# Two-layer hybrid decoder trunk: split weights of the first half kept in device memory, norm shares on another engine, two norms ended earlier

## The chip, the cores and the metric

The kernel runs on one core of one Trainium2 chip. The metric is the device time of one execution in microseconds (us), less is better. The engines named below are TensorE (PE, matmuls, with its weight loads PEld), VectorE (DVE), ScalarE (ACT), GpSimd (POOL) and SyncE (SP, which issues every DMA of this kernel). On-chip memory holds the tiles; device memory holds inputs, outputs and, after the change, some intermediate weights.

## The reference, cut to what matters

One sequence of 1024 tokens, width 1024, two layers. Layer 0 mixes with an S5 state-space block and a stick-breaking attention, layer 1 with a causal pooling; each layer then has a squared-ReLU MLP of width 4096 and a gated per-layer embedding. All in float32.

```python
for i in range(DEPTH):
    if i % 2 == 0:
        h = h + even_mixer(h, ...)     # rms_norm, h @ w_in, S5 and attention, concat @ w_out
    else:
        h = h + pool_mixer(rms_norm(h, ln_mix_odd[j]), pool_w[j], pool_scale[j])
    hn = rms_norm(h, ln_mlp[i])
    h = h + jnp.square(jax.nn.relu(hn @ w_mlp_up[i])) @ w_mlp_down[i]
    gate = jax.nn.sigmoid(rms_norm(h, ln_ple[i]) @ w_ple_gate[i])
    h = h + (p[i] @ w_ple_up[i]) * gate
```

## The kernel before

**Tiles.** Features lie on the 128 partitions, tokens along the free axis, in two halves of 512 tokens (`hf` 0 and 1). An activation is eight tiles of 128x512, a weight a tile of 128x1024 (512 KB).

**Split weights.** A float32 product is made of three matmuls in a reduced format: each operand is a high part and a low part, and `gemm` runs high x high, low x high and high x low, so a weight that serves one half is 24 matmuls of 128x512. The parts are made on the chip by `split`: ACT casts the raw tile to the high part (L448), DVE subtracts it from the raw tile for the low part (L452). `wload` (L464) takes a raw tile (tag "wr", two buffers), loads it by a DMA on SP and splits it into two tiles of another tag, mostly "wh" (eight buffers, so four weights). For a stretch of the S5 work, four of these eight buffers hold its tables. Most weights of the mixers, the first block of each MLP, the gates and the pool are used once for each half, and `wload` runs once for each use: 98 splits of this kind in the profile.

**Stages.** `build` sets the order in which the work is written, by generators that are woven into each other:
- `proj_u`: norm of x and the first four column blocks of the input projection. The norm of half 0 is a sum of squares over eight tiles (`final`, then `norm_add`, L502), whose adds run on POOL ("g"); half 1's run on DVE ("v").
- `kvq(0)`, `kvq(1)`: the other twelve column blocks (`proj`), once per half, two weights ahead, beside the S5 passes (`s5`), which need many small DVE and POOL operations and DMAs of 16 pieces (`M`).
- attention (`att`), the gated S5 output (`glu`) and the output projection (`w_out`, `out_s5`).
- `mlp_all` with `mlp` and `between`: the first block of the MLP by ordinary products, the rest by seven-product (Strassen) blocks, `order7`, whose activations and weights are summed and split separately. `after(p, n)` runs behind product n of a phase; in the last phase of layer 0 it adds the embedding's norm shares of the finished tiles.
- `ple(0, (0,))`, `ple(0, (1,))` (`ple_b`): the embedding of layer 0, half by half, eight gate weights each. Where the norm factor `self.r[hf]` is None, the first step runs `preload` (an activation table) and `norm_end` (PE sum over partitions, `st`, L518, then ACT and DVE) after its gate product.
- `pool(0)`, woven into `ple_b`, then the first MLP step of layer 1 with `pool(1)` woven in, then the MLP and the embedding of layer 1.

**What sets the order.** Every engine works through its own queue in order. The queues are laid out from the written order by a scheduler, with the buffers' reuse as the limit: a load waits until the last reader of the buffer it takes is done. SP's queue is one: a DMA that waits holds up those behind it.

Of the kernel before, what the change touches and what calls it, by code (L numbers as in the profile page):

```python
# [19 lines left out]
P = 128  # L20
# [20 lines left out]
class Kern:  # L41
    def __init__(self, ctx, tc, A):
        self.tc, self.nc, self.A = tc, tc.nc, A

        self.sb = ctx.enter_context(tc.tile_pool(name="sb", bufs=1))
        self.hi = ctx.enter_context(tc.tile_pool(name="hi", bufs=1))
        self.ps = ctx.enter_context(tc.tile_pool(name="ps", bufs=1, space=PSUM))
        self.bufs = dict(t2=3, acc=2, u=26, at=8, wq=4, r0=1, r1=1, wr=2, wh=8, mm=2, z=2, b=2, av=1, st=1)
        self.n = 0
# [414 lines left out]
    def wload(self, src, K, tags=("wr", "wh"), hi_eng="a"):  # L464

        raw = self.t([P, 1024], tags[0], name="wr")
        hi, lo = (self.t([P, 1024], tags[1], F32R, name="w") for _ in range(2))
        self.nc.sync.dma_start(out=raw, in_=src)
        self.split(raw, hi, lo, hi_eng)
        return tuple(t.rearrange("p (k n) -> p k n", k=K) for t in (hi, lo))  # L470
# [90 lines left out]
    def proj_u(self):  # L561
# [14 lines left out]
        for k in range(4):  # L576
            if k == 0:
                for i in range(2):
                    nc.sync.dma_start(out=x[0][0][:, i, :], in_=self.A["x"][0][:, i, :])
                    self.final(0, i, x[0][0][:, i, :], G_EVEN, "g")  # L580
                    for j in range(2):
                        wpart(j, i)
                continue
            load(0, k)
            for i in range(2):
                self.final(0, 2 * k + i, x[0][k][:, i, :], G_EVEN, "g")
# [10 lines left out]
        for k in range(8):  # L597
            self.final(1, k, x[1][k // 2][:, k % 2, :], G_EVEN, "v")
# [224 lines left out]
    def mlp(self, i, f, halves, h, tag="at", up=()):  # L823

        nc, v = self.nc, self.nc.vector
        load = lambda m: self.wload(self.A["w_up"][i, 4 * f + m], 8)
# [21 lines left out]
        for hf in halves:  # L848
            for m in range(8):
                ps = self.p([P, HT], "mm")  # L850
                if m % 2 == 0:
                    dn = self.wload(self.A["w_down"][i, 4 * f + m // 2], 4)
# [294 lines left out]
    def mlp_rest(self, i, h, xq):  # L1147
# [6 lines left out]
        def after(p, n):  # L1154
# [55 lines left out]
    def first_up(self, i):  # L1210
        return [self.wload(self.A["w_up"][i, m], 8) for m in range(2)]
# [49 lines left out]
    def ple(self, i, halves, h):  # L1261
# [8 lines left out]
        def up(at):  # L1270
            if at < len(jobs):
                m, hf = jobs[at]
                if m // 4 not in wu:
                    wu[1] = self.wload(A["w_pu"][i, 1], 2)
# [5 lines left out]
        for at, (m, hf) in enumerate(jobs):  # L1280
            if m + 1 not in w and m < 7:
                w[m + 1] = self.wload(A["w_gate"][i, m + 1], 8)
# [21 lines left out]
    def pool(self, hf, h):  # L1304
# [7 lines left out]
        def start(m):  # L1312
            gi = m // 2
            ps = self.p([P, HT], "av")
            if m % 4 == 0:
                self.pw = self.wload(self.A["pool_w"][m // 4], 4)
# [52 lines left out]
    def build(self):  # L1369
# [9 lines left out]
        ws = self.ahead(2, [lambda c=c: self.wload(self.A["w_in"][c], 8) for _ in range(2)  # L1379
# [43 lines left out]
        ple_b = self.ple(0, (1,), h)  # L1423
        run(steps(ple_b, 1))
# [114 lines left out]
```

## Time and profile before

| | us |
|---|---|
| median of three runs | 2117.95 (2117.68 to 2119.14) |
| the profiled execution | 2119.18 |
| its span in the profile | 2117.4 |
| granted PE clock, mean over the span | 0.981 |
| HBM read / written | 129.28 MB / 4.19 MB |

In a profile row of the chain of waits the numbers are the start and the length in us, then engine, tile and line of the kernel before; a DMA row names what is loaded from where. In a row of operations the numbers after the bar are busy us and the mean of one in ns, then idle time in front of it. In a row of waits they are us in all, times, and the longest. A row of DMAs gives the count, the size and the median us from issue to landing.

### The profile page before, as it was taken

The numbers are of one execution on the slowest core, as the hardware profiler recorded it, in microseconds if no ns is written. First come the engines' busy times: TensorE is split into PE (matmuls) and PEld (weight loads), VectorE is DVE, ScalarE is ACT, GpSimd is POOL, SyncE is SP. The second block draws the span as 40 slices with busy tenths as digits, with TensorE's granted clock in tenths as the row PEclk, the third lists the DMA queues.
The fourth block names the chain that finished last, engine by engine and source line by source line (L and its number), as shares of the span: only waits on it lengthen the run. The fifth ranks groups of instructions, "written<-read, shape, count | busy, mean of one in ns | idle before, by whom it ended". The sixth has DMA issues, their size and how long they took to land.

```text
span 2117.4 us, 24722 instructions
## 1 busy us (share of the span) xinstructions
PE 2030.2 (96%) x9464; PEld 1606.6 (76%) x9464; DVE 1781.6 (84%) x2339; ACT 1176.8 (56%) x1701; POOL 131.3 (6%) x263
## 2 busy tenths in 40 slices
PE   7999899999999999999999999879999999999998
PEld 5777665666677888888888887658888888888886
DVE  8876477888778798989769978988797998879999
ACT  5233478877744645555365655533654656365662
POOL 2678000000000000000000000000000000000000
PEclk9999899999999999999999999989999999999999
DMA  5121111210141210211211131231210211210221
GB/s 174 46 64 49 56 60 50 84 47 31 41 150 50 80 50 30 80 57 36 67 60 40 52 108 60 90 111 59 70 50 30 90 40 40 80 60 31 70 70 60
DMA packets 44741, 136.24 MB, mean 64 GB/s; under 512 B 9552, under 2 KB 10704, under 8 KB 44624
## 3 DMA queue, kind: packets, MB, share of 16 engines
q1 hardware_dynamic: 44624, 134.67, 19.0%
q8 instruction: 74, 1.21, 0.2%
q14 instruction: 43, 0.35, 0.1%
HBM read 129.28 MB, written 4.19 MB: 63 GB/s over the span
## 4 chain that ended last, share of the span: by engine, by line
PE 73%; DVE 18%; ACT 4%; issue 3%; DMA 1%; POOL 0%; SPq 0%; DVEq 0%; ACTq 0%
PE mm L480 26%; PE z L480 15%; PE b L480 13%; PE av L480 7%; PE st L480 7%; DVE rz L720 3%; DVE w L452 2%; DVE zs L724 1%; DVE xgl L532 1%; PE av L750 1%; DVE acc L502 1%; PE z L703 1%; ACT na L716 1%; ACT na L717 1%; DVE win L1335 1%
## 5 line engine op out<-in xcount | busy, mean ns | idle before, releaser
L480 PE MATMUL mm<-xgh,w 128*128 128x512 f32 x880 | 288.9, 405 | 6.9 <-DVE k L642 4.4
L452 DVE TENSOR_TENSOR w<-q,w 128x1024 fp32r<-128x1024 f32 x204 | 247.2, 1219 | 0.2 <-ACT w L448 0.2
L448 ACT CAST w<-q 128x1024 fp32r<-128x1024 f32 x204 | 212.7, 1047 | 35.0 <-PE mm L480 20.4
L448 ACT CAST hsh<-H 128x1024 fp32r<-128x1024 f32 x98 | 102.2, 1046 | 196.7 <-PE st L480 82.5
L480 PEld LDWEIGHTS mm<-xgh,w 128*128 128x128 f32 x880 | 167.9, 194 | 48.4 <-issue 9.7
L480 PE MATMUL z<-xsh,w 128*128 128x512 f32 x576 | 177.7, 390 | 0.0
L480 PE MATMUL mm<-xgl,w 128*128 128x512 f32 x440 | 177.0, 402 | 0.0
L448 ACT CAST w<-wr 128x1024 fp32r<-128x1024 f32 x98 | 102.3, 1047 | 126.8 <-PE mm L480 73.1
L452 DVE TENSOR_TENSOR w<-wr,w 128x1024 fp32r<-128x1024 f32 x98 | 128.9, 1322 | 28.4 <-ACT w L448 12.2
L894 DVE TENSOR_TENSOR q<-q,q 128x1024 f32<-128x1024 f32 x114 | 137.2, 1220 | 17.2 <-DMA q<-in_w_down 11.5
L480 PE MATMUL b<-xsh,w 128*128 128x512 f32 x448 | 137.9, 389 | 0.0
L480 PE MATMUL mm<-hsh,w 128*128 128x512 f32 x448 | 137.9, 389 | 0.0
L448 ACT CAST xsh<-X 128x1024 fp32r<-128x1024 f32 x72 | 75.5, 1051 | 98.2 <-PE st L480 51.2
L452 DVE TENSOR_TENSOR hsl<-H,hsh 128x1024 fp32r<-128x1024 f32 x98 | 119.5, 1220 | 10.7 <-ACT hsh L448 10.7
L480 PEld LDWEIGHTS z<-xsh,w 128*128 128x128 f32 x576 | 108.2, 188 | 22.9 <-issue 0.5
L480 PE MATMUL mm<-xsh,w 128*128 128x512 f32 x400 | 123.6, 389 | 0.0
L452 DVE TENSOR_TENSOR xsl<-X,xsh 128x1024 fp32r<-128x1024 f32 x72 | 87.4, 1222 | 40.9 <-ACT xsh L448 40.5
L480 PE MATMUL z<-xsl,w 128*128 128x512 f32 x288 | 112.1, 389 | 0.0
L720 DVE TENSOR_TENSOR_SCAN rz<-na,rz 128x128 f32<-128x128 f32 (+7 forms) x64 | 84.7, 1347 | 27.0 <-ACT na L717 27.0
L480 PE MATMUL mm<-hidh,w 128*128 128x512 f32 x256 | 89.2, 425 | 18.0 <-DVE w L452 9.4
L452 DVE TENSOR_TENSOR xsl<-xt,xsh 128x512 fp32r<-128x512 f32 x108 | 70.1, 686 | 42.0 <-ACT xsh L448 41.9
L480 PE MATMUL b<-hsh,w 128*128 128x512 f32 x336 | 103.6, 389 | 0.0
(366 smaller groups left out, 4842.9 us busy)
## 6 DMA issues: line engine op xcount, KB each, us to landing
q<-in_w_up SPq DMA_DIRECT2D x56, 512.0 KB, 3.8
q<-in_w_down SPq DMA_DIRECT2D x56, 512.0 KB, 3.6
wr<-in_w_in SPq DMA_DIRECT2D x26, 512.0 KB, 3.6
wr<-in_w_out SPq DMA_DIRECT2D x16, 512.0 KB, 3.5
wr<-in_w_up SPq DMA_DIRECT2D x16, 512.0 KB, 3.5
wr<-in_w_down SPq DMA_DIRECT2D x16, 512.0 KB, 3.5
x<-in_x SPq DMA_DIRECT2D x15, 512.0 KB, 4.8
wr<-in_w_gate SPq DMA_DIRECT2D x15, 512.0 KB, 3.4
```

The costliest lines, as they stand in the source:

```text
L448: nc.scalar.copy(out=hi, in_=src)
L452: e.tensor_tensor(out=lo, in0=src, in1=hi.bitcast(F32), op=ALU.subtract)
L480: self.nc.tensor.matmul(ps, a, b, start=(first and n == 0 and i == 0), stop=(last and n == K - 1 and i == 2), skip_group_check=going)
L502: e.tensor_tensor(out=self.acc[hf], in0=self.acc[hf], in1=sq, op=ALU.add)
L532: self.nc.vector.scalar_tensor_tensor(out=lo, in0=x, scalar=g, in1=hi.bitcast(F32), op0=ALU.mult, op1=ALU.subtract)
L703: nc.tensor.matmul(pz[:, 0:b1 - b0], self.q[hf][pair // 2][rows, pair % 2, i * P:(i + 1) * P], self.k[b0 // HT][pair // 2][rows, pair % 2, ...
L716: nc.scalar.activation(out=na, in_=na, func=AF.Exp)
L717: nc.scalar.activation(out=na, in_=na, func=AF.Ln, bias=1.0)
L720: v.tensor_tensor_scan(out=rz[:, rev], data0=na[:, rev], data1=rz[:, rev], initial=0.0, op0=ALU.add, op1=ALU.add)
L724: v.tensor_tensor(out=zs, in0=zs, in1=rz, op=ALU.subtract)
L750: nc.tensor.matmul(self.avp[64 * o:64 * o + 64, i * P:(i + 1) * P], self.v[kb // 4 * 2 + pair // 2][:, kb % 4, cs], w[:, at * P:(at + 1) * ...
L894: (self.nc.vector if eng == "v" else self.nc.gpsimd).tensor_tensor(out=o, in0=a, in1=b, op=op)
```

## The change

Four things, in the order of the diff:

1. `wload` gets a key. The first load under a key splits as before and then stores the high and the low part to two tiles in device memory (pool `dr`). A later load under the same key fetches both parts straight into the buffers, without a raw tile, a cast or a subtraction. Keys are given to 46 weights that are loaded twice: 12 of `w_in`, 8 of `w_out`, 8 up, 8 down, 7 gates, 1 embedding, 2 pool. That adds 92 stores and turns 46 raw loads into 92 loads of parts, each 512 KB.
2. In `proj_u` the seven adds of half 0's norm go from POOL to DVE, and the raw tiles of column blocks 2 and 3 take buffers of "wq" in place of "wr".
3. The norm of half 0 for the embedding of layer 0 ends behind product 4 of the last MLP phase, with its table load, rather than behind the first gate product.
4. `build` runs one step of `ple_b`, then the table load and the end of the pool's norm for half 0, then the second step; `pool` skips its own.

```diff
+        self.dr = ctx.enter_context(tc.tile_pool(name="dr", bufs=1, space=bass.MemoryType.DRAM))
+        self.kept = {}
...
+    def wload(self, src, K, tags=("wr", "wh"), keep=None):
+
+        if keep in self.kept:
+            parts = [self.t([P, 1024], tags[1], F32R, name="w") for _ in range(2)]
+            for t, d in zip(parts, self.kept[keep]):
+                self.nc.sync.dma_start(out=t.bitcast(F32), in_=d)
+        else:
+            raw = self.t([P, 1024], tags[0], name="wr")
+            parts = [self.t([P, 1024], tags[1], F32R, name="w") for _ in range(2)]
+            self.nc.sync.dma_start(out=raw, in_=src)
+            self.split(raw, *parts)
+            if keep is not None:
+                self.kept[keep] = []
+                for t, e in zip(parts, "hl"):
+                    name = "_".join(str(x) for x in keep) + e
+                    d = self.dr.tile([P, 1024], F32, tag=name, name=name, bufs=1)
+                    self.nc.sync.dma_start(out=d, in_=t.bitcast(F32))
+                    self.kept[keep].append(d)
+        return tuple(t.rearrange("p (k n) -> p k n", k=K) for t in parts)
...
-                    self.final(0, i, x[0][0][:, i, :], G_EVEN, "g")
+                    self.final(0, i, x[0][0][:, i, :], G_EVEN)
...
-            w.append(self.wload(self.A["w_in"][j], 8, ("wr", ("at", "wq")[j - 2])))
+            w.append(self.wload(self.A["w_in"][j], 8, ("wq", ("at", "wq")[j - 2])))
...
-                w = self.wload(self.A["w_out"][4 * part + n // 2], 4, ("wr", tag))
+                w = self.wload(self.A["w_out"][4 * part + n // 2], 4, ("wr", tag), ("out", part, n // 2))
...
+            if n == 4:
+                self.preload()
+                self.norm_end(0)
             if n == 2:
-                self.r = [None, None]
+                self.r[1] = None
...
-            if m == 0:
+            if m == 0 and self.r[hf] is None:
                 self.norm_end(hf)
...
         ple_b = self.ple(0, (1,), h)
+        run(steps(ple_b, 1))
+        self.preload()
+        self.norm_end(0)
         run(steps(ple_b, 1))
         pool = self.pool(0, h[0])
```

The other keys (`w_in` in `build`, up, down, `first_up`, `w_pu`, gate, pool) are given in the same way as that of `w_out`.

**DVE at the start.** The rows are DVE's instructions in order, with the line, the operation and out<-in; `s5blk` are the small S5 tables, `xgl` the low part of the normed x, `at` and `w` low parts of weights, `acc` and `sq` the norm's sum and a tile of squares. Line numbers after the change are 15 to 20 higher. Before:

```order
L452 TENSOR_TENSOR at_84<-wr_82,at_83 128x512
L532 SCALAR_TENSOR_TENSOR xgl_87<-x_71,gain,xgh_86 128x512
L452 TENSOR_TENSOR at_81<-wr_79,at_80 128x512
L452 TENSOR_TENSOR at_84<-wr_82,at_83 128x512
L209 MEMSET s5blk_379 128x16
L210 MEMSET s5blk_379 128x16
L83 CAST identb<-ident 128x128
L532 SCALAR_TENSOR_TENSOR xgl_89<-x_72,gain,xgh_88 128x512
```

After the change, from the same subtraction on:

```order
L455 TENSOR_TENSOR at_86<-wr_84,at_85 128x512
L547 SCALAR_TENSOR_TENSOR xgl_89<-x_73,gain,xgh_88 128x512
L517 TENSOR_TENSOR acc_98<-acc_98,sq_109 128x512
L455 TENSOR_TENSOR at_83<-wr_81,at_82 128x512
L455 TENSOR_TENSOR at_86<-wr_84,at_85 128x512
L547 SCALAR_TENSOR_TENSOR xgl_91<-x_74,gain,xgh_90 128x512
L517 TENSOR_TENSOR acc_98<-acc_98,sq_121 128x512
L547 SCALAR_TENSOR_TENSOR xgl_91<-x_74,gain,xgh_90 128x512
L517 TENSOR_TENSOR acc_98<-acc_98,sq_126 128x512
L455 TENSOR_TENSOR w_153<-wr_151,w_152 128x1024
L455 TENSOR_TENSOR w_159<-wr_157,w_158 128x1024
```

The adds into `acc` stand between the weights and the normed tiles, the two whole-weight subtractions of blocks 2 and 3 have moved up, and the S5 tables begin behind them.

**SP in the input projection.** Before, the second half's loads are raw (`wr`), behind the sixteen pieces of an S5 block:

```order
L364 DMA M_1262<-kt_1247 16x4x32 x2
L364 DMA M_1262<-kt_1247 16x4x16 x2
L468 DMA wr_1534<-in_w_in 128x1024
L468 DMA wr_1660<-in_w_in 128x1024
L468 DMA wr_1740<-in_w_in 128x1024
L468 DMA wr_1812<-in_w_in 128x1024
```

After the change, first the place where half 0's last parts are stored between raw loads (`in_4h` is the stored high part of column block 4), then that of the second half's loads:

```order
L483 DMA in_15h<-w_1194 128x1024
L476 DMA wr_1341<-in_w_in 128x1024
L483 DMA in_15l<-w_1195 128x1024
L476 DMA wr_1426<-in_w_in 128x1024
L483 DMA in_4h<-w_1342 128x1024
L483 DMA in_4l<-w_1343 128x1024
```

```order
L367 DMA M_1678<-kt_1663 16x4x32 x2
L367 DMA M_1678<-kt_1663 16x4x16 x2
L472 DMA w_1788<-in_9h 128x1024
L472 DMA w_1789<-in_9l 128x1024
L472 DMA w_1858<-in_10h 128x1024
L472 DMA w_1859<-in_10l 128x1024
L472 DMA w_1946<-in_11h 128x1024
L472 DMA w_1947<-in_11l 128x1024
```

A store stands behind the split of its weight, and raw loads written later stand behind the store; in the second half each weight is two loads.

**PE at the embedding of half 1 and the first pooled half.** `st` is the sum over partitions that ends a norm, `av` the pool's product, `mm` a gate product. Before, the norm's row comes behind the second gate weight and the pool's first six products:

```order
L480 MATMUL mm_10204<-xgl_9583,w_10127 128x512
L480 MATMUL av_10247<-xgh_9772,w_10249 128x512
L480 MATMUL av_10247<-xgh_9772,w_10250 128x512
L480 MATMUL av_10247<-xgl_9773,w_10249 128x512
L480 MATMUL av_10247<-xgh_9772,w_10249 128x512
L480 MATMUL av_10247<-xgh_9772,w_10250 128x512
L480 MATMUL av_10247<-xgl_9773,w_10249 128x512
L518 MATMUL st_10260<-acc_9782,one 128x512
L480 MATMUL mm_10311<-xgh_9584,w_10199 128x512
```

After the change it stands between the first and the second gate weight, without a product of the pool ahead:

```order
L495 MATMUL mm_10220<-xgh_9640,w_10183 128x512
L495 MATMUL mm_10220<-xgh_9640,w_10184 128x512
L495 MATMUL mm_10220<-xgl_9641,w_10183 128x512
L533 MATMUL st_10285<-acc_9848,one 128x512
L495 MATMUL mm_10299<-xgh_9642,w_10216 128x512
L495 MATMUL mm_10299<-xgh_9642,w_10217 128x512
L495 MATMUL mm_10299<-xgl_9643,w_10216 128x512
```

Then pool(1), beside the first up weights of the MLP of layer 1. Before, one up weight lies between the MLP's norm and the pool's first product (the row of the norm is 25 rows earlier):

```order
L480 MATMUL mm_10772<-xgh_10299,w_10712 128x512
L480 MATMUL mm_10772<-xgl_10300,w_10711 128x512
L480 MATMUL av_10803<-xgh_10186,w_10805 128x512
L480 MATMUL av_10803<-xgh_10186,w_10806 128x512
L480 MATMUL av_10803<-xgl_10187,w_10805 128x512
L480 MATMUL av_10803<-xgh_10186,w_10805 128x512
L480 MATMUL av_10803<-xgh_10186,w_10806 128x512
L480 MATMUL av_10803<-xgl_10187,w_10805 128x512
L518 MATMUL st_10816<-acc_10196,one 128x512
L480 MATMUL mm_10858<-xgh_10293,w_10717 128x512
```

After the change the pool's first product follows that norm's row directly:

```order
L495 MATMUL mm_10871<-xgh_10434,w_10799 128x512
L495 MATMUL mm_10871<-xgl_10435,w_10798 128x512
L533 MATMUL st_10856<-acc_10438,one 128x512
L495 MATMUL av_10902<-xgh_10272,w_10903 128x512
L495 MATMUL av_10902<-xgh_10272,w_10904 128x512
L495 MATMUL av_10902<-xgl_10273,w_10903 128x512
L495 MATMUL av_10902<-xgh_10272,w_10903 128x512
L495 MATMUL av_10902<-xgh_10272,w_10904 128x512
L495 MATMUL av_10902<-xgl_10273,w_10903 128x512
L533 MATMUL st_10913<-acc_10282,one 128x512
L495 MATMUL mm_10955<-xgh_10428,w_10808 128x512
```

The 24 matmuls of the second up weight moved from in front of the pool's first product to behind it.

More of the change, by code (lines that the diff above doesn't have):

```diff
@@ L462, in act @@
         return out
[L464 to L470, printed above, removed]
+    def wload(self, src, K, tags=("wr", "wh"), keep=None):
[16 more added lines that the diff above has]
+        return tuple(t.rearrange("p (k n) -> p k n", k=K) for t in parts)
     def gemm(self, ps, w, m, x, first=True, last=True, turn=0, going=False):
@@ L585, in proj_u @@
             for i in range(2):
-                self.final(0, 2 * k + i, x[0][k][:, i, :], G_EVEN, "g")
+                self.final(0, 2 * k + i, x[0][k][:, i, :], G_EVEN)
         w = [tuple(t.rearrange("p (k n) -> p k n", k=8) for t in hl[1:]) for hl in w]
         for j in (2, 3):
-            w.append(self.wload(self.A["w_in"][j], 8, ("wr", ("at", "wq")[j - 2])))
+            w.append(self.wload(self.A["w_in"][j], 8, ("wq", ("at", "wq")[j - 2])))
         self.consts()
@@ L597, in proj_u @@
         for k in range(8):
-            self.final(1, k, x[1][k // 2][:, k % 2, :], G_EVEN, "v")
+            self.final(1, k, x[1][k // 2][:, k % 2, :], G_EVEN)
         for j in range(4):
@@ L825, in mlp @@
         nc, v = self.nc, self.nc.vector
-        load = lambda m: self.wload(self.A["w_up"][i, 4 * f + m], 8)
+        load = lambda m: self.wload(self.A["w_up"][i, 4 * f + m], 8, keep=("up", i, m))
         n_up = 2 if tag == "wh" else 4
@@ L851, in mlp @@
                 if m % 2 == 0:
-                    dn = self.wload(self.A["w_down"][i, 4 * f + m // 2], 4)
+                    dn = self.wload(self.A["w_down"][i, 4 * f + m // 2], 4, keep=("down", i, m // 2))
                 self.gemm(ps, dn, m % 2, hid[hf])
@@ L1210, in first_up @@
     def first_up(self, i):
-        return [self.wload(self.A["w_up"][i, m], 8) for m in range(2)]
+        return [self.wload(self.A["w_up"][i, m], 8, keep=("up", i, m)) for m in range(2)]
     def between(self, i, solo):
@@ L1273, in up @@
                 if m // 4 not in wu:
-                    wu[1] = self.wload(A["w_pu"][i, 1], 2)
+                    wu[1] = self.wload(A["w_pu"][i, 1], 2, keep=("pu", 1))
                 ups.append(self.p([P, HT], "zb"[at // 2 % 2]))
@@ L1281, in ple @@
             if m + 1 not in w and m < 7:
-                w[m + 1] = self.wload(A["w_gate"][i, m + 1], 8)
+                w[m + 1] = self.wload(A["w_gate"][i, m + 1], 8, keep=("gate", m + 1))
             hk = h[hf][m]
@@ L1315, in start @@
             if m % 4 == 0:
-                self.pw = self.wload(self.A["pool_w"][m // 4], 4)
+                self.pw = self.wload(self.A["pool_w"][m // 4], 4, keep=("pool", m // 4))
             wt = [t[:, 2 * (gi % 2):2 * (gi % 2) + 2] for t in self.pw]
             self.gemm(ps, wt, m % 2, xg[2 * gi:2 * gi + 2])
-            if m == 0:
+            if m == 0 and self.r[hf] is None:
                 self.norm_end(hf)
@@ L1377, in build @@
         self.k, self.q, self.v = [[], []], [[], []], []
-        ws = self.ahead(2, [lambda c=c: self.wload(self.A["w_in"][c], 8) for _ in range(2)
+        ws = self.ahead(2, [lambda c=c: self.wload(self.A["w_in"][c], 8, keep=("in", c)) for _ in range(2)
                             for c in (8, 9, 10, 11, 12, 13, 14, 15, 4, 5, 6, 7)])
```

## Prediction

> **What bounds the kernel now.** I read three views in this order: the page with the busy shares and the chain that ended last, then the busy time by stage, then the chain and the waits inside the stages that are not saturated.
>
> ```profile
> span 2117.4 us, 24722 instructions
> PE 2030.2 (96%) x9464; PEld 1606.6 (76%) x9464; DVE 1781.6 (84%) x2339; ACT 1176.8 (56%) x1701; POOL 131.3 (6%) x263
> PE 73%; DVE 18%; ACT 4%; issue 3%; DMA 1%; POOL 0%; SPq 0%; DVEq 0%; ACTq 0%
> ```
>
> TensorE (PE) is busy for 96% of the span, but only 73% of the chain is PE; VectorE (DVE) holds 18% and ScalarE (ACT) 4%. So there are stretches in which the PE goes at the pace of the others. The view by stage says where (columns: start and end, length, then busy us and instructions of PE, weight load, DVE, ACT, POOL, then granted clock, DMA share, GB/s):
>
> ```profile
> 0.00:80.00 80.00, 62.97 (x248) 48.53 (x249) 72.31 (x254) 32.53 (x50) 29.68 (x53) 0.97 0.35 120
> 80.00:250.00 170.00, 159.31 (x929) 121.80 (x927) 112.64 (x158) 55.58 (x84) 100.74 (x203) 0.93 0.20 62
> ...
> 420.00:590.00 170.00, 157.36 (x912) 110.53 (x911) 139.00 (x156) 130.91 (x205) 0.00 (x0) 0.98 0.15 51
> 590.00:660.00 70.00, 65.79 (x277) 52.97 (x276) 62.09 (x78) 31.09 (x42) 0.00 (x0) 0.95 0.36 126
> 660.00:1270.00 610.00, 610.00 (x2687) 503.68 (x2686) 519.80 (x602) 339.67 (x457) 0.23 (x2) 1.00 0.18 58
> 1270.00:1350.00 80.00, 72.36 (x297) 56.14 (x296) 72.91 (x109) 44.71 (x74) 0.67 (x6) 0.96 0.20 67
> 1350.00:1410.00 60.00, 48.59 (x172) 34.89 (x171) 54.05 (x77) 26.14 (x46) 0.00 (x0) 0.88 0.28 92
> 1410.00:1460.00 50.00, 45.19 (x176) 35.11 (x175) 43.45 (x52) 17.83 (x22) 0.00 (x0) 0.90 0.35 121
> 1460.00:2100.00 640.00, 637.87 (x2808) 526.48 (x2807) 560.21 (x656) 354.04 (x479) 0.00 (x0) 1.00 0.16 55
> ```
>
> From 660 to 1270 the PE is never idle: 610.00 us over 2687 matmuls is 0.227 us each at a clock of 1.00. From 1460 on it is the same. Nothing in these 1250 us can be won by freeing DVE or ACT. Measured by 0.227 us a matmul, the others lose: 590 to 660, 277 matmuls are worth 63 us, so 7 are lost; 1270 to 1350, 297 are worth 67, 13 lost; 1350 to 1410, 172 are worth 39, 21 lost; 1410 to 1460, 176 are worth 40, 10 lost. DVE is at 72.91 of 80 and 54.05 of 60 in the two stages that lose most: there it is the bound. Before 590 the shapes are mixed, and I go by the chain.
>
> **The change, price of one reload.** A first use is loaded raw, cast on ACT and subtracted on DVE. 46 second uses lose both operations and get two 512 KB loads instead of one: 12 of the input projection, 8 each of the output projection, up and down, 7 gates, 1 of the embedding, 2 of the pool.
>
> ```profile
> L448 ACT CAST w<-wr 128x1024 fp32r<-128x1024 f32 x98 | 102.3, 1047 | 126.8 <-PE mm L480 73.1
> L452 DVE TENSOR_TENSOR w<-wr,w 128x1024 fp32r<-128x1024 f32 x98 | 128.9, 1322 | 28.4 <-ACT w L448 12.2
> wr<-in_w_in SPq DMA_DIRECT2D x26, 512.0 KB, 3.6
> out_h<-x SPq DMA_DIRECT2D x15, 256.0 KB, 2.0
> 36.00:38.00 2.00, 2.00 (x11) 1.65 (x10) 2.00 (x5) 2.00 (x5) 0.00 (x0) 1.00 1.02 418
> ```
>
> Of these 98 splits, 46 go: 46 x 1.05 = 48 us of ACT and 46 x 1.32 = 61 us of DVE. What it costs: today a split waits for a free pair of buffers with its raw tile already landed, so a weight is ready 1.05 + 1.32 = 2.4 us after its buffers come free; afterwards the whole transfer comes behind that moment. If the two halves follow each other strictly it is 2 x 3.6 = 7.2 us; if the second only adds its bytes, 3.6 + 0.52 MB at the 418 GB/s of the last row, 1.25, gives 4.9. A weight is 24 matmuls, 24 x 0.227 = 5.44 us of PE. So where one other weight covers the reload, the price lies between 0 and 7.2 - 5.44 = 1.8 us for each, 83 us for 46. By the nearest row, the single load's 3.6, I take the lower end for most, and four reloads at 1.8, **+7 us**: those for which the order leaves no other weight ahead (the pool's first weight, which now follows one norm row after the gemm whose buffers it takes over, and those of the input projection while four of the eight buffers hold S5 tables).
>
> The Trainium skill, page "DMA: Bandwidth & Descriptors", section "Anatomy of one DMA — SWDGE (gpsimd) path", fits a transfer by 2.0 us + bytes / 436 GB/s. As an estimate, that page gives 4.4 us for both halves together and no stall, and a total 7 us lower than mine; its 3.2 us for one half is below the 3.6 us of the row, so the measurement decides and the term stays.
>
> **The start, 0 to 80.**
>
> ```profile
> L502 POOL TENSOR_TENSOR acc<-acc,sq x7: 1266/1327/1938, 8.3 to 21.8; 128x512 f32<-128x512 f32 x7
> L502 DVE TENSOR_TENSOR acc<-acc,sq x77: 673/685/693, 34.5 to 2013.9; 128x512 f32<-128x512 f32 x77
> 12.37 1.21 DVE s5blk L122
> ...
> 22.43 1.18 DVE s5blk L131
> 24.96 0.17 DVE L124 TENSOR_SCALAR s5blk<-s5blk 128x16 f32<-128x16 f32 x1
> PE mm L480 <- DVE k L642: 4.4, 1, 4.4
> ```
>
> Between 12.37 and 22.43 the chain holds six small S5 operations of about 1.2 us, while POOL runs its seven adds; after the adds the same form takes 0.17. Moving the adds removes 6 x 1.03 = 6 us of stretching and adds 7 x 0.685 = 4.8 us to DVE. In the new order 25 fewer of the small operations stand ahead of the first key result, for which the PE waits 4.4 us: 25 x 0.17 = 4.2. Two raw tiles of this projection that now come from another tag lose a wait for an earlier split; where DVE is the bound that brings nothing. Net 4.8 - 6 - 4.2, about **-5 us**. Bounds: -10 (the adds fall in gaps) and +5 (DVE waited for x under the stretched operations anyway).
>
> **Second half of the input projection and attention, 80 to 590.**
>
> ```profile
> 185.03 1.14 DVE w L452
> 206.32 0.94 ACT w L448
> 208.03 1.27 DVE w L452
> 265.12 1.12 DVE w L452
> 283.94 1.22 DVE w L452
> ...
> 581.38 1.14 DVE w L452
> 582.54 3.50 DMA wr<-in_w_out
> ```
>
> The first five pieces of the chain are splits of second uses, 5.7 us; I take **-4**, since behind each stands another DVE operation. At the end of the attention a split and the raw load behind it are 4.6 us of the chain, and splits also stand in front of attention copies in ACT's queue: **-5**. Bounds together: -14, and +29 if all 16 reloads there cost 1.8.
>
> **Output projection and first MLP blocks, 590 to 660.** 12 second uses leave DVE, 12 x 1.32 = 16 us of 62.09, but only the 7 lost PE microseconds can come back: **-5**, bounds -7 and +22 (12 x 1.8). The embedding of half 0 lies in the saturated stretch; its earlier norm, which issues no DMA, is worth 0 there, because PE has other matmuls to run.
>
> **Embedding of half 1 with the pool, 1270 to 1460.**
>
> ```profile
> 1282.39 1.23 DVE w L452
> 1307.54 3.38 DMA wr<-in_w_gate
> 1350.04 4.71 DMA wr<-in_w_down
> 1448.06 4.50 DMA wr<-in_w_down
> PE av L480 <- DVE pz L1326: 4.9, 3, 4.5
> L1291 ACT ACT_TABLE_LOAD x3 | 3.8, 1283 | 0.1
> 1410.00:1460.00 50.00, 13.26 (x11) 0.90 0.35 121
> ```
>
> In the first stage DVE sheds six splits that fall inside it, 6 x 1.22 = 7.3 us; the norm, now taken before the second step, removes the 4.5 us wait for pz from the front but only hands the PE on to a full DVE. With two more table loads of 1.28 us on an ACT that idles 35 of 80 us (cost nothing; 2.6 if in the norm's own path), **-7**, bounds -13 and +14 (8 reloads). In the second the chain waited 4.71 us for a raw down load, held back by splits that had not freed its buffer; two pool and two up splits go and free it earlier: **-4**, bounds -12 and +7. In the third, of the 13.26 us of splits in 11 operations (last row, DVE busy in this stage at line 452) most are second uses, yet the load of 4.50 us comes with them: **-5**, bounds -10 and +11.
>
> **The sum.** -5 - 4 - 5 - 5 - 7 - 4 - 5 = -35, +7 for reloads = -28. The profiled execution took 2119.2 us for its span of 2117.4, so 2091; the median of the runs is 2118.0, 1.2 below it, and gives **2090 us**.
>
> **The rivals.**
>
> *The reloads come late (slower).* The buffer pair comes free when its last matmul ends, and two transfers then stand before the next weight. For it: 7.2 us exceed the 5.44 of one weight. Against it: eight buffers hold four weights, so outside the S5 stretch two or three weights lie between. It eats the gain of 35 from 35 / 1.8 = 19 of 46 reloads on; with 30 of them, 54 us, it is 2118 - 35 + 54 = 2137.
>
> *The stores hold things up (slower).* Each first use is now followed by two 512 KB stores on the same queue, which wait for the split, and later raw loads stand behind them; the pair of buffers is also not free before both have landed. A 256 KB store took 2.0 us, so two of 512 KB last at least 4.0 and, at the load's 3.6, 7.2: the same 1.8 over the PE's 5.44. With 30 of 46: again 54 us, less the net 28, so 2144; it decides from 28 / 1.8 = 16. Against it: with PE saturated the DMA share is 0.16 to 0.18, so the room is there, and a first use is gone through in no less than 5.44 us anyway. The 2.0 us of the 256 KB store, below the 3.6 of a 512 KB load, shows no long tail at a store's end. The Trainium skill, in the same page and section ("DMA: Bandwidth & Descriptors", "Anatomy of one DMA — SWDGE (gpsimd) path"), says that a transfer's completion is slowest where the target is device memory, which speaks for this rival; that row bears it out so little that its chance is small.
>
> *Only the DVE-bound stages gain.* The splits before 660 had slack that the chain doesn't show, their reloads cost what they save; 1270 to 1350 and 1410 to 1460 remain, -7 - 5 = -12: 2106.
>
> *The PE takes it up.* The splits on the chain are replaced by the next DVE operation, and reload stalls offset the rest: within 4 us of 2118.
>
> *More than the sum.* In 1270 to 1460 the PE was busy for 166 us with matmuls worth 146 at full clock, at granted clocks of 0.96, 0.88 and 0.90. If fewer gaps raise the clock, up to 20 us more: 2070.
>
> **How the numbers follow.** Forecast 0.44 (2078 to 2100), only the DVE-bound stages 0.19, more than the sum 0.14, the PE takes it up 0.10, reloads late 0.08, stores 0.05. The range runs from 2066 to 2120: it takes in the DVE-bound case and the unchanged one, and leaves out the two slow cases and the far end of the gain, under 0.2. The bounds of the single terms all added reach further on both sides, but no one mechanism puts all of them at one end. About 0.2%, 4.2 us, is what a measurement of this kernel can tell from no change: faster 0.77, same 0.10, slower 0.13.
>
> **What would show it.** Right: splits at 52 for 98; from 1270 on, the stages that sum to 190 us take about 174; no DMA wait of 4.7 at the first down block; the small S5 operations near 12 us at 0.17; first keys some 5 us sooner. Wrong: PE or DVE waits ended by a reload in many places, a row of PE waits of 1 to 2 us in the second projection, or raw loads that are issued late behind stores. If the stretch before 590 ends no sooner and only the later one does, the DVE-bound rival holds.

## The result and the profile after

| kernel | median us | lowest to highest | runs | ratio to before, 95% interval |
|---|---|---|---|---|
| before, beside these runs | 2118.14 | 2115.79 to 2119.14 | 6 | |
| changed | 2099.77 | 2092.86 to 2100.92 | 6 | 0.9904 [0.989, 0.9919] |

The change saves 18.4 us, 28 were forecast. The profiled execution is the fastest of the six, 2092.86 us for a span of 2090.8, and so 7 us away from the median; the others are within 1.2 us of each other. Where those 7 us lie is part of what follows.

The page of the changed kernel (the lines that answer to those of before):

```profile
span 2090.8 us, 24861 instructions
PE 2018.7 (97%) x9464; PEld 1602.4 (77%) x9464; DVE 1740.8 (83%) x2300; ACT 1134.4 (54%) x1658; POOL 116.2 (6%) x256
HBM read 153.40 MB, written 52.43 MB: 98 GB/s over the span
PE 79%; DVE 14%; ACT 4%; issue 2%; SPq 1%; DMA 0%; POOL 0%; DVEq 0%; ACTq 0%
wr<-in_w_in SPq DMA_DIRECT2D x14, 512.0 KB, 5.7
```

PE's share of the chain went from 73% to 79%, DVE's from 18% to 14%: as meant, splits left the path. The price is in the other rows: 48 MB more are written (52.43 against 4.19) and 24 MB more read, and a raw load of the input projection, now sharing the queue with stores, takes 5.7 us to land where it took 3.6 (3.7 in `no_keep_in` below, which neither stores nor reloads the input projection's weights).

The splits that are left, from the groups of line 455 (count, then shortest, median and longest in ns, first and last start):

```profile
L455 DVE TENSOR_TENSOR w<-wr,w x52: 1198/1221/6278, 14.1 to 1394.4; 128x1024 fp32r<-128x1024 f32 x52
```

98 became 52. The median is 1.22 us, before as after; the 1.32 that the forecast used is a mean, raised by a few long ones. Then the waits of PE that the reloads end (us in all, times, longest), whole span:

```profile
PE mm L495 <- DVE s5blk L214: 6.5, 1, 6.5
...
PE mm L495 <- DMA w<-in_9h: 1.9, 1, 1.9
...
PE av L495 <- DMA w<-pool_0h: 1.7, 1, 1.7
...
PE av L495 <- DMA w<-pool_0l: 0.8, 1, 0.8
...
PE mm L495 <- DMA w<-in_9l: 0.5, 1, 0.5
```

PE waits for only two of 46 reloads, 1.9 + 0.5 and 1.7 + 0.8, 4.9 us in all. Both are where the forecast put them: the pool's first weight and one of the input projection.

For the stages I take marks that both kernels have. Before, the first key result, the first operation of the Strassen blocks, the first and last pooled output, the last add of the first MLP block (first and last start in each row):

```profile
L642 DVE TENSOR_TENSOR k<-mm,r x8: 677/682/691, 77.7 to 223.8; 128x512 f32<-128x512 f32 x8
L925 DVE SCALAR_TENSOR_TENSOR xt<-X,X x96: 681/684/692, 653.6 to 1908.7; 128x512 f32<-128x512 f32 x96
L1326 DVE SCALAR_TENSOR_TENSOR pz<-av,gain,r x16: 740/745/753, 1290.2 to 1400.3; 128x512 f32<-128x512 f32 x16
L854 DVE TENSOR_TENSOR x<-x,mm x32: 661/685/690, 572.4 to 1474.2; 128x512 f32<-128x512 f32 x32
```

and after:

```profile
L657 DVE TENSOR_TENSOR k<-mm,r x8: 676/684/692, 72.9 to 223.0; 128x512 f32<-128x512 f32 x8
L940 DVE SCALAR_TENSOR_TENSOR xt<-X,X x96: 680/684/693, 637.6 to 1881.5; 128x512 f32<-128x512 f32 x96
L1344 DVE SCALAR_TENSOR_TENSOR pz<-av,gain,r x16: 737/746/752, 1273.8 to 1378.7; 128x512 f32<-128x512 f32 x16
L869 DVE TENSOR_TENSOR x<-x,mm x32: 660/682/690, 563.3 to 1447.0; 128x512 f32<-128x512 f32 x32
```

Lead of the changed kernel at these marks: 4.8 us at the first key, 16.0 at the Strassen blocks, 16.4 at the first pooled output, 21.6 at the last, 27.2 at the last add, and from there on it stays within 1 us of that. The same marks and a few more, read in each profile, give the stages (us):

| stage | before | changed | changed, again | stored parts only | no stored parts | norms undone |
|---|---|---|---|---|---|---|
| to the first key | 77.7 | 72.9 | 73.1 | 77.7 | 72.0 | 71.8 |
| to the last query | 235.5 | 234.7 | 234.5 | 239.6 | 234.7 | 234.8 |
| to the end of attention | 276.1 | 271.8 | 276.2 | 274.6 | 285.8 | 271.9 |
| to the last output projection | 25.9 | 24.9 | 24.9 | 25.0 | 25.8 | 24.9 |
| to the first Strassen operation | 38.4 | 33.3 | 33.3 | 33.3 | 38.5 | 33.3 |
| to the first Strassen result | 102.6 | 101.2 | 101.4 | 101.2 | 101.6 | 101.4 |
| to the last embedding output, half 1 | 594.4 | 588.8 | 588.4 | 589.9 | 594.2 | 589.8 |
| to the last pooled output | 49.7 | 51.1 | 53.1 | 46.8 | 51.4 | 46.8 |
| to the last add of the first MLP block | 73.9 | 68.3 | 69.5 | 68.6 | 73.2 | 68.7 |

The rows from 25.9 down repeat from kernel to kernel; the two above them do not: the attention of one and the same program took 271.8 and 276.2.

### The profile page after: what moved, and what is told of

Read it like the earlier page. It is cut to its first block, busy times and chain, and to the rows that moved or that the text cites. A ratio compares the mean times of both kernels' runs of the same rounds, so it can differ in the third digit from the quotient of the medians.

```text
span 2090.8 us, 24861 instructions
## 1 busy us (share of the span) xinstructions
PE 2018.7 (97%) x9464; PEld 1602.4 (77%) x9464; DVE 1740.8 (83%) x2300; ACT 1134.4 (54%) x1658; POOL 116.2 (6%) x256
## 3 DMA queue, kind: packets, MB, share of 16 engines
HBM read 153.40 MB, written 52.43 MB: 98 GB/s over the span
## 4 chain that ended last, share of the span: by engine, by line
PE 79%; DVE 14%; ACT 4%; issue 2%; SPq 1%; DMA 0%; POOL 0%; DVEq 0%; ACTq 0%
PE mm L495 29%; PE z L495 15%; PE b L495 13%; PE av L495 7%; PE st L495 7%; DVE rz L735 3%; DVE zs L739 1%; PE av L765 1%; PE z L718 1%; DVE w L455 1%; ACT na L731 1%; PE z L432 1%; PE z L505 1%; DVE win L1353 1%; ACT na L732 1%
## 5 line engine op out<-in xcount | busy, mean ns | idle before, releaser
L495 PE MATMUL mm<-xgh,w 128*128 128x512 f32 x880 | 283.9, 401 | 13.5 <-DVE s5blk L214 6.5
L495 PE MATMUL z<-hsh,w 128*128 128x512 f32 x336 | 104.0, 390 | 0.0
L495 PEld LDWEIGHTS mm<-xgl,w 128*128 128x128 f32 x440 | 84.2, 191 | 19.3 <-DVE xgl L547 1.4
L495 PEld LDWEIGHTS mm<-hsh,w 128*128 128x128 f32 x448 | 84.1, 188 | 17.5
```

The source lines that it names most:

```text
L495: self.nc.tensor.matmul(ps, a, b, start=(first and n == 0 and i == 0), stop=(last and n == K - 1 and i == 2), skip_group_check=going)
```

## The experiments

Two theories stood against each other. Mine: the stored parts carry the gain, the start some 5 us, the norms next to nothing. The rival: start and norms carry it, and the reloads cost what the splits did. The runs stand in one table; all but the first six of the changed kernel were made in three groups, each with its own runs of before (44 together).

| kernel | median us | runs | ratio to before, 95% interval | mean clock | mean us at clock 0.983 |
|---|---|---|---|---|---|
| before, in the three groups | 2119.9 | 44 | | 0.9809 | 2116.7 |
| changed | 2099.8 | 6 | 0.9904 [0.989, 0.9919] | 0.9830 | 2098.9 |
| after_again | 2100.3 | 5 | 0.9904 [0.9888, 0.9921] | 0.9820 | 2098.2 |
| no_keep | 2119.9 | 12 | 1.0 [0.9987, 1.0013] | 0.9798 | 2115.3 |
| keep_only | 2101.9 | 5 | 0.9911 [0.9894, 0.9928] | 0.9824 | 2100.3 |
| no_keep_in | 2094.1 | 4 | 0.9875 [0.9856, 0.9894] | 0.9852 | 2096.6 |
| keep_in_only | 2121.5 | 12 | 1.0008 [0.9993, 1.0023] | 0.9792 | 2115.0 |
| in_store_only | 2101.5 | 6 | 0.9928 [0.9909, 0.9946] | 0.9817 | 2101.6 |
| norms_undone | 2088.2 | 5 | 0.9865 [0.9844, 0.9885] | 0.9856 | 2093.8 |
| norms_undone_2 | 2092.5 | 6 | 0.986 [0.9833, 0.9887] | 0.9852 | 2095.2 |
| no_in_no_pool | 2100.5 | 6 | 0.9913 [0.9893, 0.9932] | 0.9825 | 2099.7 |
| norms_undone_no_in | 2092.5 | 4 | 0.9862 [0.9834, 0.9889] | 0.9855 | 2096.0 |
| late_norm_undone | 2094.5 | 4 | 0.9874 [0.9851, 0.9898] | 0.9840 | 2095.8 |
| pool_adds | 2105.2 | 6 | 0.9922 [0.9901, 0.9943] | 0.9825 | 2103.8 |

The last column: every run states the mean clock granted to the PE. Within the kernels' own runs the time falls by 1.41 us for each 0.001 of clock (correlation -0.93 over all runs, each kernel's mean taken off). Each kernel's mean is moved along that line to 0.983. This takes out the scatter, but also whatever of the clock belongs to a kernel; the medians hold both. The clock is stated to 0.001, so differences of 1 to 2 us in this column are not to be relied on.

### The changed kernel again: where the 7 us lie

No edit.

> The changed kernel, unaltered. The first six times were 2092.86 for the profiled execution and 2099.73 to 2100.92 for the other five. If the profiled one had a higher granted clock by chance (0.987 against 0.981 to 0.983), this run's times scatter between 2092 and 2101 and follow the clock; if it was another placement or chip, they stay near one value, and the profile shows in which stage the 7 us lie.

It came to 2100.3, profile included (2098.2 us of span, clock 0.981). Up to the last query the two profiles are equal (307.6 us); then the attention takes 271.8 in one and 276.2 in the other. One stretch of it in the first profile (PE, PEld, DVE, ACT, POOL busy, then granted clock, DMA share, GB/s):

```profile
500.00:520.00 20.00, 18.17 (x105) 13.67 (x105) 17.11 (x21) 16.05 (x25) 0.00 (x0) 1.00 0.00 1
```

and in the second:

```profile
500.00:520.00 20.00, 19.81 (x102) 14.56 (x101) 15.91 (x21) 15.74 (x25) 0.00 (x0) 0.85 0.00 1
```

The same program, the same DMA silence, a clock of 1.00 or 0.85. The stage table has the 7 us in three stages in which the PE has gaps, 4.4 in the attention, 2.0 in the pool and 1.2 behind it, and in each the second profile has the lower clock (0.97 for 0.99, 0.87 for 0.93, 0.93 for 0.95). What sets the clock was not tried. The first profile was a lucky one; a sum made from it alone would have said that 28 was hit to within 2.

### Stored parts alone, and all but the stored parts

`no_keep` takes the keys away, `keep_only` takes all else away:

```diff
+        keep = None
         if keep in self.kept:
```

```diff
-                    self.final(0, i, x[0][0][:, i, :], G_EVEN)
+                    self.final(0, i, x[0][0][:, i, :], G_EVEN, "g")
...
-            w.append(self.wload(self.A["w_in"][j], 8, ("wq", ("at", "wq")[j - 2])))
+            w.append(self.wload(self.A["w_in"][j], 8, ("wr", ("at", "wq")[j - 2])))
...
-            if n == 4:
-                self.preload()
-                self.norm_end(0)
             if n == 2:
-                self.r[1] = None
+                self.r = [None, None]
...
-        run(steps(ple_b, 1))
-        self.preload()
-        self.norm_end(0)
         run(steps(ple_b, 1))
```

> Keeps the start and the two norm moves, but every use is loaded raw and split again. My theory, that the stored parts carry most of the gain: slower than the changed kernel by 13 to 25 us, so 2110 to 2118, or 0 to 8 faster than before. The rival, that start and norms carry it and the reloads only cost what they save: within 4 us of 2100.

> The kernel before with the stored parts alone: adds on POOL, raw tiles of blocks 2 and 3 in their old tag, norms where they were. My theory: 10 to 20 us faster than before, 2098 to 2108, since the start's 5 us and what the norms bring are missing. The rival: within 4 us of before, 2118.

2119.9 and 2101.9: without the stored parts the change gives nothing measurable, with them alone all but 2 us of it. At equal clock the stored parts are worth 16.8 us with the rest (2115.3 against the 2098.5 between the two sets of the changed kernel) and 16.4 without it (2116.7 against 2100.3). The stage table says where: with stored parts 33.3 for 38.4 up to the Strassen blocks, 588.4 to 589.9 for 594.4 up to the end of the embedding, 46.8 for 49.7 in the pool, 68.6 for 73.9 behind it. The rival is out. But if start and norms were worth 5 us or more, `no_keep` should have shown it, and the start alone is ahead by 5.7 at the first key there. Something gives it back.

### The norms

`norms_undone` is the changed kernel with the third and the fourth part of the diff above taken back; `late_norm_undone` takes back only the fourth (that in `build`):

```diff
         run(steps(ple_b, 1))
-        self.preload()
-        self.norm_end(0)
-        run(steps(ple_b, 1))
         pool = self.pool(0, h[0])
```

> The changed kernel with both norms ended where they were before. The forecast gave them nothing in the saturated stretch and the removal of one wait of 4.5 us in front of a full VectorE. My theory: 0 to 4 us slower than the changed kernel, 2100 to 2104. The rival, that they are what makes room for the reloads in the later stages: 8 us slower or more.

> The kernel with both norms where they were, a second time, on another chip. The first gave 2088.2 in the median, 12 us under the changed kernel, of which its profile shows 3 to 5 us between the first saturated block and the end of the pool; the rest went with a higher granted clock (0.986 against 0.982). If the clock is chance: 2091 to 2097. If it belongs to the kernel: 2086 to 2091.

> The changed kernel with only the later norm, the one between the first two steps of the embedding of half 1, back where it was; the earlier one stays behind product 4. If the later one costs the 3 to 5 us, by what it does to the order behind it: 2088 to 2096, and the profile has about 636 us from the first saturated block to the end of the pool. If the earlier one does: 2098 to 2101 and about 640 us.

2088.2 and 2092.5 against 2100: I had expected the opposite sign. The norm moves cost the kernel 7 to 12 us in the medians and 4 at equal clock. With only the later one undone it is 2094.5. From the first Strassen result to the last pooled output the profiles have 639.9 and 641.5 us with both moves, 636.6 and 636.9 without, 637.0 with only the later undone: 3 to 5 us, and the later move has nearly all of them.

The loss shows in the second pooled half. The view of the last stage but one, changed kernel:

```profile
1327.60:1378.70 51.10, 42.34 (x162) 30.78 (x162) 43.23 (x63) 23.99 (x42) 0.00 (x0) 0.93 0.46 164
```

changed kernel, again:

```profile
1331.80:1384.90 53.10, 45.38 (x161) 32.91 (x161) 43.22 (x62) 24.05 (x42) 0.00 (x0) 0.87 0.44 159
```

norms undone, and the later norm undone:

```profile
1327.90:1374.70 46.80, 40.76 (x168) 30.39 (x166) 42.49 (x61) 22.43 (x40) 0.00 (x0) 1.00 0.45 164
```

```profile
1337.20:1384.10 46.90, 40.86 (x168) 30.45 (x166) 42.59 (x63) 22.47 (x40) 0.00 (x0) 1.00 0.47 166
```

The busy time of DVE is the same to 1 us (42.5 to 43.2), so DVE was not relieved of work; the clock is 1.00 without the move and 0.93 or 0.87 with it. The order in time at that place, changed kernel, PE and then DVE (start, length):

```profile
1332.96 1.02 PE L533 MATMUL st<-acc,one 128*128 128x512 f32 x2
1335.70 0.49 PE L495 MATMUL av<-xgh,w 128*128 128x512 f32 x1 [1.72 <-DMA w<-pool_0h]
1336.97 0.50 PE L495 MATMUL av<-xgh,w 128*128 128x512 f32 x1 [0.78 <-DMA w<-pool_0l]
...
1338.23 1.10 PE L533 MATMUL st<-acc,one 128*128 128x512 f32 x2
1340.12 0.73 PE L495 MATMUL mm<-xgh,w 128*128 128x512 f32 x2 [0.79 <-DVE relu L855]
```

```profile
1321.85 1.29 DVE L1367 SCALAR_TENSOR_TENSOR x<-win,x 128x512 f32<-128x512 f32 x2
...
1338.65 0.69 DVE L528 TENSOR_TENSOR r<-r,ra 128x512 f32<-128x512 f32 x1
...
1346.51 0.74 DVE L1344 SCALAR_TENSOR_TENSOR pz<-av,gain,r 128x512 f32<-128x512 f32 x1
```

and norms undone:

```profile
1325.92 1.12 PE L533 MATMUL st<-acc,one 128*128 128x512 f32 x2 [0.95 <-DVE acc L517]
1333.49 1.12 PE L533 MATMUL st<-acc,one 128*128 128x512 f32 x2 [0.96 <-DVE ra L526]
1335.57 0.70 PE L495 MATMUL mm<-xgh,w 128*128 128x512 f32 x2 [0.96 <-DVE relu L855]
```

```profile
1315.11 0.69 DVE L1364 SCALAR_TENSOR_TENSOR x<-win,x 128x512 f32<-128x512 f32 x1
...
1333.93 0.69 DVE L528 TENSOR_TENSOR r<-r,ra 128x512 f32<-128x512 f32 x1
...
1343.38 0.74 DVE L1341 SCALAR_TENSOR_TENSOR pz<-av,gain,r 128x512 f32<-128x512 f32 x1
```

With the move, PE's order there is: the products of the first two up weights (48 matmuls from 1315.33 on), the sum for the MLP's norm (the first `st`), the pool's first six products, the sum for the pool's norm, and then the product of the third up weight. Without the later move, in both kernels that lack it, the MLP's sum stands between the first and the second up weight, and the pool's first products stand behind both sums. So the reading of pool(1) in the section on the change was wrong: the `mm` rows behind the pool's sum wait for a `relu`, which reads an earlier product, and so are those of the third up weight. The second did not move behind the pool's product, it moved in front of the MLP's sum.

What is late is the norm factor `r` of the MLP. The first row of DVE in each view is the last pooled `x` of half 0: it ends at 1323.14 with the move and at 1315.80 without. The sum needs it and stands 7 us later, at 1332.96 for 1325.92, and the factor comes at 1338.65 for 1333.93. In both kernels the third up product waits for a `relu` that needs this factor, and starts at 1340.12 for 1335.57. Counted from the last embedding output, it starts 12.3 to 13.9 us on in all six profiles with the later move and the later weights stored, and 7.6 to 7.7 us on in all five that have these weights stored without the later move. The 5 us between them are about the loss of the stage (51.1 to 54.3 for 46.8 to 47.0). That the first pooled half ends later because its pool begins one gate step later is likely and was not tried, nor was why the scheduler lays it out so. The lower clock comes with it; its share was not separated. What the move saves at its own place, 1.1 us up to the embedding's end (588.8 for 589.9 with the stored parts alone), is less than this.

### The pool's reload

The rival for the last point was the reload itself. `no_in_no_pool` loads the pool's weights raw again, and has no keys for the input projection either:

```diff
+        keep = None if keep and keep[0] in ("in", "pool") else keep
         if keep in self.kept:
```

> The changed kernel without the keys of the input projection and of the pool, whose first reload the PE waited for, 1.7 and 0.8 us. If that stall is on the path and two splits more are not: 1 to 3 us faster than without the input keys alone, 2091 to 2093. If VectorE's full stage is the bound there, the two splits put back cost 2 us and it is the same or slower, 2094 to 2097.

2100.5, no better than the changed kernel. The stage of the pool, 54.3 us here, is longer still:

```profile
1332.90:1387.20 54.30, 44.40 (x161) 32.67 (x161) 45.33 (x65) 26.25 (x44) 0.00 (x0) 0.87 0.37 134
```

DVE has 2 us more to do and the clock is at 0.87. The wait for the reload is gone, and the third up product starts as late as before, 12.3 us into the stage, with a longer wait for `relu` in its place:

```profile
1345.23 1.22 PE L496 MATMUL mm<-xgh,w 128*128 128x512 f32 x2 [1.80 <-DVE relu L856]
```

`late_norm_undone` keeps the reload, does not wait for it, and has 46.9 us. So what costs is the late norm factor, not the reload.

### The keys of the input projection

`no_keep_in` leaves out those twelve keys, `keep_in_only` has only them, `in_store_only` stores the parts but loads raw in the second half, `norms_undone_no_in` has neither those keys nor the norm moves:

```diff
-        ws = self.ahead(2, [lambda c=c: self.wload(self.A["w_in"][c], 8, keep=("in", c)) for _ in range(2)
+        ws = self.ahead(2, [lambda c=c: self.wload(self.A["w_in"][c], 8) for _ in range(2)
```

```diff
+        keep = keep if keep and keep[0] == "in" else None
         if keep in self.kept:
```

```diff
+        if keep in self.kept and keep[0] == "in":
+            keep = None
         if keep in self.kept:
```

> The changed kernel without the twelve keys of the input projection: 24 stores and 12 pairs of loads less, 12 splits more. By the forecast's term of 4 us it is 4 us slower, 2104. By the trace of the changed kernel, in which that stage took 235 us as before and a wait for a reload behind an S5 block stood in the chain, the reloads cost what the splits did: within 2 us of the changed kernel. If the stores and reloads harm what stands beside them, faster by 2 to 6 us.

> Start and norms as in the changed kernel, but of the stored parts only the twelve of the input projection. If these keys cost some 6 us by themselves, as their removal from the changed kernel suggests: 4 to 8 us over the kernel without any stored parts, which was within 3 us of before, so 2122 to 2130. If they are neutral and the 6 us came from the scatter of the clock: within 3 us of before, 2117 to 2123.

> The changed kernel, in which the twelve weights of the input projection are still stored in the first half but loaded raw and split in the second, so the stores stay and the late reloads go. If the reloads behind the S5 blocks are what costs 6 us: as without the keys, 2092 to 2097. If the 24 stores hold up the raw loads and buffers: as the changed kernel, 2098 to 2103.

> Both norms where they were and no keys for the input projection. If the two parts are independent and worth 4 to 6 us each: 2083 to 2088, the best so far. If the 6 us without those keys were the clock's scatter, as the two runs of the same program in that stage (229.7 and 240.8 us) suggest: as with the norms undone alone, 2088 to 2096.

The first run, 2094.1, was 6 us under the changed kernel and looked like a finding. The other pairs took it back. With only these keys the kernel is 1.6 over the one with none (2121.5 and 2119.9); without them but with the norms undone it is 2092.5, where the same kernel with them was 2088.2 and 2092.5. At equal clock the three pairs give 2 in favour of leaving them out, 0.3 and 1.5 in favour of the keys: nothing. The stores without the reloads came to 2101.5; at equal clock that is 5 us over no keys at all, which would make the stores a cost that the reloads win back, but it rests on one pair with few runs and stays open. How far chance goes in this stage is seen in two kernels that have the same number of instructions there on every engine and differ only in the keys of the pool's weights, which come later, `no_keep_in` and `no_in_no_pool` (first key to last query):

```profile
71.70:301.40 229.70, 219.19 (x1273) 163.90 (x1274) 158.70 (x255) 107.75 (x173) 101.47 (x203) 0.95 0.21 63
```

```profile
71.90:312.70 240.80, 226.94 (x1273) 169.92 (x1274) 159.66 (x255) 107.81 (x173) 100.64 (x203) 0.92 0.19 60
```

11 us apart with the same work, at a clock of 0.95 and 0.92. No stage time from one profile can settle a question of 4 us there.

One thing that the twelve keys cost is seen in the chain of the changed kernel:

```profile
189.85 0.53 SPq L472
190.48 4.11 DMA w<-in_9l
```

and in the order in time of SP's queue (start, length):

```profile
178.40 11.35 SPq L367 DMA_DIRECT2D M<-kt  x16
189.85 0.53 SPq L472 DMA_DIRECT2D w<-in_9h  x1
```

The same block of pieces, the third of four, before:

```profile
150.66 16.80 SPq L468 DMA_DIRECT2D wr<-in_w_in  x3
167.66 10.16 SPq L364 DMA_DIRECT2D M<-kt  x16
```

The sixteen pieces of an S5 block hold SP for 11 us; the reload of block 9 stands behind them and lands 4.11 us after its issue, and the PE waits 2.4 us for it. Before, three of the twelve raw loads of the second half stand ahead of this block of pieces; after, only the reload of block 8 does. That the reload's buffers come free later is the likely reason, and was not tried. The 2.4 us explain part of the missing 4; where the rest went is not shown.

### The start

`pool_adds` puts the seven adds back on POOL and leaves the raw tiles in the new tag:

```diff
-                    self.final(0, i, x[0][0][:, i, :], G_EVEN)
+                    self.final(0, i, x[0][0][:, i, :], G_EVEN, "g")
```

> The changed kernel with the seven adds of the first norm back on POOL, the raw tiles left in their new tag. If the stretch of the small operations by the adds is what costs the 5 us at the start: first key result at 77 to 78 us in place of 73, and 3 to 7 us slower, 2103 to 2107. If it was the loads that no longer wait: first key result at 73 to 74 and no slower.

2105.2, 5 us over the changed kernel, and the first key result at 77.3:

```profile
L657 DVE TENSOR_TENSOR k<-mm,r x8: 679/692/692, 77.3 to 229.1; 128x512 f32<-128x512 f32 x8
```

So the adds are what counts, not the loads. I had priced six stretched S5 operations. In this kernel's order only one small S5 operation falls beside POOL's adds, but other operations of DVE do, and they are stretched in its place (last row: the small one):

```profile
17.47 1.78 DVE L547 SCALAR_TENSOR_TENSOR xgl<-x,gain,xgh 128x512 fp32r<-128x512 f32 x1
19.18 1.31 DVE L86 CAST identb<-ident 128x128 bf16<-128x128 f32 x1
...
22.25 1.25 DVE L127 TENSOR_SCALAR s5blk<-s5blk 128x16 f32<-128x16 f32 x1
```

With the adds on DVE the first two of these forms take 0.74 and 0.22 us. From 12.82 to 23.43 two more `xgl` and two splits are stretched as well; together these operations lose some 5.7 us against the changed kernel, close to the 6 that were priced. What comes late by it is the first norm factor:

```profile
34.77 0.69 DVE L528 TENSOR_TENSOR r<-r,ra 128x512 f32<-128x512 f32 x1
```

for the adds on POOL, and with the adds on DVE

```profile
30.98 0.68 DVE L528 TENSOR_TENSOR r<-r,ra 128x512 f32<-128x512 f32 x1
```

(37.39 before). POOL's last four adds took 1.75 us each, where DVE needs 0.685 (`pool_adds`):

```profile
16.48 7.00 POOL L517 TENSOR_TENSOR acc<-acc,sq 128x512 f32<-128x512 f32 x4
```

But they end at 23.48, and DVE's seven adds of the changed kernel end at 23.49: the sum of squares is not late. Late are the last two `xgl` of half 0, at 26.37 and 27.60 for 20.88 and 22.15, and behind them on PE the sum over partitions, at 29.1 for 24.8. And 76 operations on the S5 tables stand ahead of the factor on DVE, where the changed kernel has 27 (81 before). That the adds cost 5 us is shown; the stretched operations and the small ones in front are both in the trace, and how the 5 us divide between them was not tried.

As to `no_keep`, -5 from the start and +4 from the norms would make -1, and 2116.7 to 2115.3 at equal clock is what it has. Its own profile bears this out only in part: 5.7 us ahead at the first key, but only 1.5 behind from the first Strassen result to the last pooled output (645.6 for 644.1; `keep_in_only` has 648.3), with the third up product 11.1 us into the pool's stage for 9.1 before, and 9.7 behind in the attention, the stage that scatters.

## Why the prediction was right, and where it was not

Sign and range held: 2099.8 lies between 2066 and 2120. But it lies at the very edge of the forecast's own 2078 to 2100, and nearer to the 2106 of the rival in which only the DVE-bound stages gain than to 2090. That rival is half right: up to the end of the attention the stored parts brought nothing that can be told from chance. It is wrong from there to the Strassen blocks, where 6 us were won (25.9 to 24.9 and 38.4 to 33.3). The size was two thirds of the forecast, -18.4 for -28. At equal clock, 16.4 to 16.8 from the stored parts and 5 from the start, less 4 for the norms, make the 18 that were measured (2116.7 to 2098.5). Term by term:

- **Stored parts.** Forecast, without the start: -30 for the stages and +7 for reloads, 23 saved. Measured: 16.4 and 16.8 at equal clock. Three terms hold by the stage table: 590 to 660, -5 forecast, 38.4 to 33.3; 1410 to 1460, -5 forecast, 73.9 to 68.6; the reloads, +7 forecast, 4.9 of PE waits, at the two places named. The embedding was -7, and 594.4 to 589.9 is -4.5.
- **Second half of the input projection, -4.** This step failed: nothing, by three pairs. The pieces of the chain were splits, and one of them gave way to a reload behind the S5 pieces in SP's queue. The forecast counted such reloads among the stalls at 1.8 us; it did not see that one of them stands in the chain of the very stage that was to gain. With 2.4 us of wait that is part of the miss, and the rest stays open.
- **Attention, -5.** Eleven profiles with stored output weights took 271.8 to 276.4, before 276.1, the two others without them 277.9 and 285.8. Some gain, not separable from the clock.
- **The pool's second half, -4.** This is the step that failed most: with the stored parts alone it is -2.9 (49.7 to 46.8), with the whole change +1.4 (51.1), +3.4 in the second profile. The forecast had the new order in front of it, misread which up weight had moved, and priced the new neighbourhood of norm row and pool product as one reload stall. The stall was real, 2.5 us, but without the reload the stage took 54.3. The price was the MLP's norm factor, 5 us later into the stage behind a first pooled half that ended later, and a clock of 0.93 for 1.00.
- **The norms, 0 and part of -7.** The wait of 4.5 us for `pz` did go, but not by the norm moves. The row in `no_keep`, which has the moves, and in `keep_only`, which has none:

```profile
PE av L496 <- DVE pz L1345: 5.0, 4, 4.5
```

```profile
PE av L495 <- DVE pz L1341: 0.2, 1, 0.2
```

  The stored parts took it away. What the moves delayed behind themselves costs 4 us, so the kernel is better without them: 2088.2 and 2092.5, ratios 0.9865 and 0.986 to before, faster than the kernel before and the changed one. The intervals (at most 0.9887) lie just below those of the changed kernel (from 0.9888 up).
- **The start, -5.** 4.8 at the first key, 5.2 at equal clock: right in size. Of its mechanism, both parts are in the trace, the stretch beside POOL's adds and the small operations that moved behind; the stretched operations are not the ones named, once the order has changed. Their shares were not measured, so the exact hit is partly luck. The PE, ahead at the first key, waits 6.5 us for the S5 tables next (no such wait before), and the stage behind the first key is only 0.8 us shorter than before.
- **Chances.** "Reloads late" and "stores" were rightly small: two waits. The rival that a higher clock adds up to 20 us had something right: the clock rose from 0.93 to 1.00 ahead of the Strassen blocks, from 0.90 to 0.93 in the second pooled half and from 0.91 to 0.95 behind it. But this came within the gains of these stages and not on top of them, and without the norm moves the pooled half had 1.00. The rival of the DVE-bound stages added up the wrong pair: by the forecast's own rows DVE is fullest from 1270 to 1410, which would give 2107 and not 2106.

## What to carry to other kernels

Parts that are made twice can be stored and fetched, where an engine other than the PE sets the pace and the fetch stands in a queue with nothing slow ahead of it; where it stands behind a block of small DMAs, part of its gain is gone. When a step is moved ahead, look at what is late two stages on: the cost of the norm moves was not where they were put, but later, where the next norm waited for the pool's first half. Where the time follows the granted clock, note the clock of each run beside its time, and judge an edit by several kernels that differ in it, not by one pair.

## What the runs showed of the hardware

The scatter between runs of one kernel goes with the PE's clock: 44 runs of before lie between 2112.2 us (clock 0.985) and 2125.3 (0.977), about 1.4 us for each 0.001. It falls only in stages in which the PE has gaps; in the saturated stretch, read from 850 to 1150 us, every profile has 1.00. Two stretches with the same work differed by 11 us in 230. While POOL ran a 128x512 add, single operations of DVE beside it took up to 1.1 us more than without: 1.31 for 0.22, 1.78 for 0.74, 1.25 for 0.17.
